# A decoder layer on one core: rotation tables moved from GpSimd to VectorE, operand splits made on 128 partitions, and the lower-part products put last in each step

## The chip, the core and the metric

The kernel runs on one core of one Trainium2 chip. The core has TensorE (matrix products into PSUM, "PE" in the profile, with its weight loads as "PEld"), VectorE ("DVE"), ScalarE ("ACT"), GpSimd ("POOL") and a queue of SyncE ("SP") that issues most of the transfers from HBM. Each engine takes its own instructions in order and waits on semaphores for the others. The metric is the device time of one execution in microseconds, the median of three runs.

## The reference

The reference is one layer of a hybrid decoder for 256 positions and 2048 channels, in float32. One projection `x @ w_in` feeds three token mixers, whose results are gated, merged and projected; two layer norms and a squared-ReLU MLP with 8192 hidden channels follow.

```python
h = jnp.einsum('bsd,dn->bsn', x, w_in)          # 2048 -> 14352 columns
y_a = s5_branch(...)                            # 64 groups of 16 channels, 64 complex states each
y_b = gla_branch(...)                           # 4 heads, chunked gated linear attention
y_c = hgrn2_branch(...)                         # 8 heads, the same with another gate
merged = sum_b sigmoid(gate_b) * (y_b @ w_up_b);  mix = merged @ w_out
x = layer_norm(ALPHA * x + mix);  x = layer_norm(ALPHA * x + square(relu(x @ w1)) @ w2)
```

The part that the change touches most is the S5 branch. Each state p of a group follows s_t = a s_(t-1) + (Bbar u)_t with a complex a = mag * exp(i * theta), and y = Re(C s) + D u. With the state written as a rotation times a slowly varying z, the recurrence becomes a real one: z_t = mag * z_(t-1) + exp(-i theta t) (Bbar u)_t, and s_t = exp(i theta t) z_t. That needs tables of cos(theta t) and sin(theta t) for every state and all 256 positions.

## The kernel before, in words

**Products.** Every large product is made of float32 operands split in two: an upper part rounded to the type `float32r`, and a lower part, the rest. A product is then upper x upper + upper x lower + lower x upper. ScalarE makes the upper part of the weights (`emit_split`, an ACTIVATE at line 129 on a page of 128 x 1024), VectorE the lower (`emit_lower`, a TENSOR_TENSOR at line 107, the raw page less the upper one). The weights come in units of 512 KB, one page each, up to 8 units ahead (`AHEAD`), and each unit is used in two consecutive steps. The split of a unit is placed `LA` = 6 steps ahead of its use.

**Steps.** The program is one list of 1140 steps. A step of kind "rows" has the activations as stationary operand and two 128-deep slices of the unit as moving operand (128 x 512): six matmuls, lines 1341 (upper x upper), 1342 (upper x lower part of the weights) and 1343 (lower x upper). A step of kind "cols" has the weights as stationary operand: per 128-deep slice one matmul of the weights' upper part with both parts of the activations side by side (line 1346, 512 columns) and one of the weights' lower part with the activations' upper part (line 1347, 256 columns), four slices to a step; a kind "low" has the same pairs. There are 752 "rows" steps, 384 "cols" and 4 "low".

**What is woven in.** Everything else (S5, the two attentions, the norms) is written as tasks that are stepped between the steps. `run_tasks(1240, 1240)` lets a task emit instructions only while the estimated VectorE and ScalarE time already emitted (`used`) is under a budget that grows by 1240 ns each step. So the order of the instructions on every engine is fixed by these estimates when the program is built; work on GpSimd is not counted in them. The order on an engine is the order of emission.

**S5.** The 32 pairs of groups are handled in 16 half-blocks `hb` of two. `s5_prepare` scales B and C, transposes them on PE, and copies the result from PSUM into `W` (ScalarE). For each half-block it gathers the inputs `u` and the B rows into stacks of 96 partitions (`RU`, `RB`: three copies of 32 rows each, 12 transfers on SP, lines 463 and 464). ScalarE rounds the stacks (`SU`, `SB`), and VectorE replaces the second third of `SU` and the last third of `SB` by the lower parts (two operations on 32 partitions x 512). One matmul over the 96 rows then is the three-part product (`pb`, line 519: four matmuls of 256 columns).

`s5_tables(hb)` makes cos and sin of all 256 positions from 16 fine and 16 coarse angles by the addition theorems: six operations of 128 x 512 on GpSimd (lines 493 to 498: two products and a difference for the cosine, two products and a sum for the sine). `s5_main` calls it for the next half-block when the matmuls of this one have been issued. Then VectorE rotates `pb` by the tables (eight operations of 128 x 256 at line 107 and two of 128 x 512), scans four rows of 256 (line 543), rotates back, and PE multiplies by C (line 563).

## Time and profile before

| | |
|---|---|
| median of three runs | 1694.33 us (1694.15 to 1695.88) |
| the profiled execution: device time | 1696.22 us |
| the profiled execution: span from first to last instruction | 1694.4 us |
| PE busy | 1671.3 us, 99% of the span, 9396 matmuls |
| VectorE busy | 1190.8 us, 70% |
| ScalarE busy | 825.5 us, 49% |
| GpSimd busy | 161.3 us, 10%, in the first 800 us |
| from HBM | 308.7 MB, 183 GB/s over the span |

An engine's busy share is an average over stages. The matmuls are pipelined: the profile gives each a duration of about 0.39 us, but the next one starts about 0.23 us after it, so what one matmul costs is read from the starts of two neighbours and not from the duration. A wait is put down to the engine and line that ended it. "Granted clock" is the share of TensorE's full clock in a stretch of time.

### The profile page before, as it was taken

To read this page: it belongs to the slowest core of one execution; us is meant where nothing else is said; L and a number is where in the kernel's file an instruction comes from. 1 tells how busy PE (TensorE), PEld (TensorE's weight loads), DVE (VectorE), ACT (ScalarE), POOL (GpSimd) and SP (SyncE) were. 2 spreads that over 40 slices of the span, in tenths; PEclk is the share of its full clock that TensorE was granted. 3 is DMA by queue.
4 is the path that set the end of the run, shared out by engine and by line. 5 is a ranking of instruction groups with operands and counts; after the bars stand their busy time and mean duration, and the time that the engine had idled before them with its cause. 6 is when DMAs were issued, how large, how long until landed. Compare 5 with 4: busy or idle time off the path is not lost.

```text
span 1694.4 us, 24226 instructions
## 1 busy us (share of the span) xinstructions
PE 1671.3 (99%) x9396; PEld 1386.1 (82%) x9396; DVE 1190.8 (70%) x1587; ACT 825.5 (49%) x1166; POOL 161.3 (10%) x121
## 2 busy tenths in 40 slices
PE   9999999999999999999999999999999999999997
PEld 7887788887877877788888888888888888888886
DVE  6968778797998999985575667545555545555556
ACT  5553554564644434435554466454454545464550
POOL 3222022012332332200000000000000000000000
PEclk9999999999999999999999999999999999999999
DMA  9945655564555665676676545655656565656561
GB/s 287 275 145 157 178 177 168 153 194 139 173 180 169 194 196 172 207 221 186 200 263 220 187 150 150 197 188 187 211 179 206 163 213 171 218 163 208 197 233 50
DMA packets 222900, 318.70 MB, mean 188 GB/s; under 512 B 13205, under 2 KB 122129, under 8 KB 222785
## 3 DMA queue, kind: packets, MB, share of 16 engines
q1 hardware_dynamic: 217488, 308.59, 58.3%
q10 hardware_dynamic: 4528, 7.31, 1.3%
q0 software_dynamic: 768, 1.25, 0.5%
q8 instruction: 74, 1.21, 0.3%
q14 instruction: 42, 0.34, 0.1%
HBM read 308.71 MB, written 2.10 MB: 183 GB/s over the span
## 4 chain that ended last, share of the span: by engine, by line
PE 66%; DVE 4%; issue 1%; ACT 0%; DVEq 0%
PE acc L1341 15%; PE acc L1342 15%; PE acc L1343 15%; PE acc L1346 14%; PE acc L1347 7%; DVE pg L107 2%; DVE hf L107 1%; PE m L134 1%; DVE hf L543 1%; PE m L563 1%; DVE pg L118 0%; PE pb L519 0%; ACT pg L129 0%; DVE st L941 0%; DVEq L1403 0%
## 5 line engine op out<-in xcount | busy, mean ns | idle before, releaser
L129 ACT ACTIVATE pg<-pg 128x1024 fp32r<-128x1024 f32 (+2 forms) x604 | 603.1, 1028 | 413.7 <-PE acc L1342 147.0
L107 DVE TENSOR_TENSOR pg<-pg,pg 128x1024 fp32r<-128x1024 f32 (+3 forms) x646 | 749.9, 1188 | 58.9 <-ACT pg L129 32.7
L1341 PE MATMUL acc<-pg,pg 128*128 128x512 f32 x1504 | 595.5, 396 | 2.7 <-DVE pg L107 1.8
L1342 PE MATMUL acc<-pg,pg 128*128 128x512 f32 x1504 | 587.3, 390 | 2.7 <-DVE pg L107 2.7
L1343 PE MATMUL acc<-pg,pg 128*128 128x512 f32 x1504 | 587.0, 390 | 0.2
L1346 PE MATMUL acc<-pg,pg 128*128 128x512 f32 x1552 | 551.9, 400 | 0.0
L1347 PE MATMUL acc<-pg,pg 128*128 128x256 f32 x1552 | 436.6, 281 | 1.9 <-DVE pg L107 1.9
L1346 PEld LDWEIGHTS acc<-pg,pg 128*128 128x128 f32 x1552 | 292.4, 188 | 72.9 <-issue 0.7
L1341 PEld LDWEIGHTS acc<-pg,pg 128*128 128x128 f32 x1504 | 282.8, 188 | 68.4 <-issue 5.8
L1343 PEld LDWEIGHTS acc<-pg,pg 128*128 128x128 f32 x1504 | 282.6, 188 | 61.5 <-DVE pg L107 1.4
L1342 PEld LDWEIGHTS acc<-pg,pg 128*128 128x128 f32 x1504 | 282.9, 188 | 60.6 <-DVE pg L107 5.1
L1347 PEld LDWEIGHTS acc<-pg,pg 128*128 128x128 f32 x1552 | 293.9, 189 | 2.8 <-DVE pg L107 2.3
L129 ACT ACTIVATE hf<-acc 128x256 f32<-128x256 f32 (+2 forms) x103 | 40.0, 388 | 184.5 <-PE acc L1347 179.6
L107 DVE TENSOR_TENSOR pg<-pg,acc 128x512 f32<-128x512 f32 x56 | 38.3, 685 | 121.3 <-PE acc L1343 121.3
L107 DVE TENSOR_TENSOR hf<-acc,hf 128x256 f32<-128x256 f32 (+1 forms) x69 | 29.1, 421 | 131.9 <-ACT hf L129 131.9
L107 DVE TENSOR_TENSOR hf<-hf,hf 128x512 f32<-128x512 f32 (+1 forms) x144 | 106.6, 758 | 4.7 <-ACT hf L129 2.8
L129 ACT ACTIVATE hf<-hf 128x256 f32<-128x256 f32 (+1 forms) x152 | 67.7, 456 | 2.3 <-DMA hf<-pg 0.5
L129 ACT ACTIVATE pg<-acc 128x512 f32<-128x512 f32 x40 | 23.8, 595 | 83.7 <-PE acc L1343 74.5
L107 DVE TENSOR_TENSOR hf<-pb,hf 128x256 f32<-128x256 f32 x128 | 46.5, 414 | 22.8 <-PE pb L519 16.8
L107 DVE TENSOR_TENSOR pg<-hf,pg 128x256 fp32r<-128x256 f32 x84 | 34.7, 421 | 27.7 <-ACT pg L129 27.6
L129 ACT ACTIVATE pg<-m 128x512 fp32r<-128x512 f32 (+2 forms) x35 | 19.6, 559 | 68.0 <-PE m L134 51.8
L543 DVE TENSOR_TENSOR_SCAN hf<-p,hf 128x256 f32<-128x256 f32 x64 | 47.7, 792 | 0.0
(128 smaller groups left out, 641.1 us busy)
## 6 DMA issues: line engine op xcount, KB each, us to landing
pg<-in_w_in_dram SPq DMA_DIRECT2D x224, 512.0 KB, 4.2
pg<-in_w_mlp_in_dram SPq DMA_DIRECT2D x128, 512.0 KB, 4.6
pg<-in_w_mlp_out_dram SPq DMA_DIRECT2D x128, 512.0 KB, 4.0
pg<-in_w_up_dram SPq DMA_DIRECT2D x48, 512.0 KB, 4.7
pg<-in_w_out_dram SPq DMA_DIRECT2D x32, 512.0 KB, 5.5
pg<-in_s_w_glu_dram SPq DMA_DIRECT2D x8, 512.0 KB, 4.7
hf<-pg SPq DMA_DIRECT2D x96, 32.0 KB, 1.9
hf<-hf SPq DMA_DIRECT2D x96, 32.0 KB, 1.9
```

Of the source, the lines that this page charges most:

```text
L107: V.tensor_tensor(o, a, b, op=op)
L129: S.activation(o, a, f, **kw)
L134: T.transpose(ps[:, i * 128:(i + 1) * 128], s, ident)
L543: V.tensor_tensor_scan(z[:, i, :], S5["mag"][:, j:j + 1].to_broadcast([128, 256]), z[:, i, :], 0.0, ALU.mult, ALU.add)
L563: T.matmul(yps[r, 0:256], lhsT=W[:, 2 + ri, r], rhs=m[:, i, :], start=ri == 0, stop=ri == 1)
L1341: T.matmul(ps, lhsT=a[0][:, sl], rhs=wh[:, i, :], start=f, stop=False)
L1342: T.matmul(ps, lhsT=a[0][:, sl], rhs=wl[:, i, :], start=False, stop=False)
L1343: T.matmul(ps, lhsT=a[1][:, sl], rhs=wh[:, i, :], start=False, stop=l)
L1346: T.matmul(ps, lhsT=wh[:, i, n], rhs=a[2], start=f, stop=False)
L1347: T.matmul(ps[:, 0:256], lhsT=wl[:, i, n], rhs=a[0], start=False, stop=l)
```

## The change

Four things are changed.

1. **Products.** In each step the products with the lower part of the weights come last. In a "rows" step the order of the six matmuls was uu, ul, lu, uu, ul, lu (u upper, l lower; activations first) and is uu, lu, uu, lu, ul, ul. In a "cols" step the eight matmuls were 512, 256, 512, 256 ... columns and are four of 512 and then four of 256.
2. **Tables.** `s5_tables` is on VectorE and nothing of it on GpSimd. The fine angles go from 0.5 to 7.5 in place of 0 to 15 (`tvec` has 0.5 added; 8 of its 16 entries are used), the coarse ones are the same 16. One product pair gives the sum and the difference of two angles, so that a table of 16 x 16 is made of products of 16 x 8: per half-block eight operations of 128 x 256, four products and four sums, half of the sums written in reversed order. Places where other tasks may step in (`yield 0`) stand between them.
3. **Rotations.** `pb` holds the real parts of both groups in one buffer and the imaginary parts in the other, so the eight rotations of 128 x 256 become four of 128 x 512.
4. **Parts on 128 partitions.** `s5_prepare` splits `u` and B into upper and lower parts before the gather, on all 128 partitions, once per pair of half-blocks: two ACTIVATEs (`UP`, `BP`) and two subtractions of 128 x 256 on VectorE. The transfers fetch upper or lower rows as each third needs them. The two subtractions of 32 x 512 per half-block are gone.

The step's budget goes from 1240 to 1290 ns.

```diff
+        ts(tvec[:, 0, :], tvec[:, 0, :], 0.5, None, ALU.add)
...
+            UP = half((128, 2, 256), F32R)
+            act(UP[:, 0, :], u, AF.Copy)
...
-            W = half((128, 4, 128))
-            act(W, ps.rearrange("p (b s) -> p b s", b=4), AF.Copy)
+            W, BP = half((128, 2, 128)), half((128, 2, 256), F32R)
+            act(BP[:, 0, :], ps[:, 0:256], AF.Copy)
+            act(W, ps[:, 256:512].rearrange("p (b s) -> p b s", b=2), AF.Copy)
             S5["W", b] = W
+            yield 0.5
+            tt(UP[:, 1, :], u, UP[:, 0, :].bitcast(F32), ALU.subtract)
+            tt(BP[:, 1, :], ps[:, 0:256], BP[:, 0, :].bitcast(F32), ALU.subtract)
...
-                        nc.sync.dma_start(RU[32 * k:32 * k + 32, i, :], u[r])
-                        nc.sync.dma_start(RB[32 * k:32 * k + 32, i, :], W[r, 0:2, :].rearrange("p a b -> p (a b)"))
+                        nc.sync.dma_start(RU[32 * k:32 * k + 32, i, :], UP[r, int(k == 1), :].bitcast(F32))
+                        nc.sync.dma_start(RB[32 * k:32 * k + 32, i, :], BP[r, int(k == 2), :].bitcast(F32))
...
-                tt(SU[32:64], RU[32:64], SU[32:64].bitcast(F32), ALU.subtract)
-                tt(SB[64:96], RB[64:96], SB[64:96].bitcast(F32), ALU.subtract)
...
-        so, co, w = (half((128, 2, 16, 16)) for _ in range(3))
-        G.tensor_tensor(co, coarse(cs), fine(cs), op=ALU.mult)
-        G.tensor_tensor(w, coarse(sn), fine(sn), op=ALU.mult)
-        G.tensor_tensor(co, co, w, op=ALU.subtract)
-        G.tensor_tensor(so, coarse(sn), fine(cs), op=ALU.mult)
-        G.tensor_tensor(w, coarse(cs), fine(sn), op=ALU.mult)
-        G.tensor_tensor(so, so, w, op=ALU.add)
-        free(w)
+        so, co = half((128, 2, 16, 16)), half((128, 2, 16, 16))
+        for o, x1, y1, x2, y2, op1, op2 in ((co, cs, cs, sn, sn, ALU.subtract, ALU.add),
+                                            (so, sn, cs, cs, sn, ALU.add, ALU.subtract)):
+            w = half((128, 2, 2, 16, 8))
+            tt(w[:, 0], coarse(x1), fine(y1), ALU.mult)
+            tt(w[:, 1], coarse(x2), fine(y2), ALU.mult)
+            yield 0
+            tt(o[:, :, :, 8:16], w[:, 0], w[:, 1], op1)
+            tt(o[:, :, :, 7::-1], w[:, 0], w[:, 1], op2)
+            free(w)
+            yield 0
...
-                    T.matmul(pb[i][:, ri, :], lhsT=SB[:, i, ri * 128:(ri + 1) * 128], rhs=SU[:, i, :],
+                    T.matmul(pb[ri][:, i, :], lhsT=SB[:, i, ri * 128:(ri + 1) * 128], rhs=SU[:, i, :],
...
-            for i in range(2):
-                tt(zr[:, i, :], pb[i][:, 0, :], cs[:, i, :], ALU.mult)
-                tt(w1[:, i, :], pb[i][:, 1, :], sn[:, i, :], ALU.mult)
+            tt(zr, pb[0], cs, ALU.mult)
+            tt(w1, pb[1], sn, ALU.mult)
...
-        run_tasks(1240, 1240)
+        run_tasks(1290, 1290)
...
-                T.matmul(ps, lhsT=a[0][:, sl], rhs=wh[:, i, :], start=f, stop=False)
-                T.matmul(ps, lhsT=a[0][:, sl], rhs=wl[:, i, :], start=False, stop=False)
-                T.matmul(ps, lhsT=a[1][:, sl], rhs=wh[:, i, :], start=False, stop=l)
-            elif c.kind == "cols" or i // (nj // 2) == t:
-                T.matmul(ps, lhsT=wh[:, i, n], rhs=a[2], start=f, stop=False)
-                T.matmul(ps[:, 0:256], lhsT=wl[:, i, n], rhs=a[0], start=False, stop=l)
+            for i, kt in kts:
+                a = c.act(kt)
+                T.matmul(ps, lhsT=a[0][:, sl], rhs=wh[:, i, :], start=kt == 0, stop=False)
+                T.matmul(ps, lhsT=a[1][:, sl], rhs=wh[:, i, :], start=False, stop=False)
+            for i, kt in kts:
+                T.matmul(ps, lhsT=c.act(kt)[0][:, sl], rhs=wl[:, i, :], start=False, stop=kt == nk - 1)
+        else:
...
+            for i, kt in kts:
+                T.matmul(ps, lhsT=wh[:, i, n], rhs=c.act(kt)[2], start=kt == 0, stop=False)
+            for i, kt in kts:
+                T.matmul(ps[:, 0:256], lhsT=wl[:, i, n], rhs=c.act(kt)[0], start=False, stop=kt == nk - 1)
```

How the program's order moves is shown at two places. The first is the first "cols" step on PE. `acc` is the accumulator, the second name (`pg_112`, `pg_144`) the activations with both parts, `pg_368` the upper and `pg_369` the lower part of the weights. Before:

```order
L1346 MATMUL acc_406<-pg_112,pg_368 128x512
L1347 MATMUL acc_406<-pg_112,pg_369 128x256
L1346 MATMUL acc_406<-pg_112,pg_368 128x512
L1347 MATMUL acc_406<-pg_112,pg_369 128x256
L1346 MATMUL acc_406<-pg_144,pg_368 128x512
L1347 MATMUL acc_406<-pg_144,pg_369 128x256
L1346 MATMUL acc_406<-pg_144,pg_368 128x512
L1347 MATMUL acc_406<-pg_144,pg_369 128x256
```

And with the change, the same step and the one after it:

```order
L1355 MATMUL acc_414<-pg_112,pg_368 128x512 x2
L1355 MATMUL acc_414<-pg_144,pg_368 128x512 x2
L1357 MATMUL acc_414<-pg_112,pg_369 128x256 x2
L1357 MATMUL acc_414<-pg_144,pg_369 128x256 x2
L1355 MATMUL acc_424<-pg_112,pg_368 128x512 x2
L1355 MATMUL acc_424<-pg_144,pg_368 128x512 x2
L1357 MATMUL acc_424<-pg_112,pg_369 128x256 x2
L1357 MATMUL acc_424<-pg_144,pg_369 128x256 x2
```

The first use of the lower part moves from the second to the fifth place of a step, and short matmuls follow short ones.

The second place is VectorE in the middle of S5, in the stage where the attentions are over: one half-block's rotations, scans and the lower parts of the weights between them (`pg_...<-pg_...,pg_...` of 128 x 1024; the scans are written SCALAR_TENSOR_TENSOR with `p`, and `pg_4852`, `pg_5159` belong to the merge). Before:

```order
L107 TENSOR_TENSOR hf_6127<-pb_0_6110,hf_5779 128x256
L107 TENSOR_TENSOR hf_6127<-pb_1_6111,hf_5779 128x256
L107 TENSOR_TENSOR hf_6126<-hf_6126,hf_6127 128x512
L107 TENSOR_TENSOR pg_6167<-pg_5995,pg_6166 128x1024
L543 SCALAR_TENSOR_TENSOR hf_6125<-p_602,hf_6125 128x256 x2
L107 TENSOR_TENSOR pg_6188<-pg_6038,pg_6187 128x1024
L107 TENSOR_TENSOR hf_6198<-hf_6096,hf_6198 32x512
L107 TENSOR_TENSOR hf_6199<-hf_6097,hf_6199 32x512
L107 TENSOR_TENSOR pg_6212<-pg_6056,pg_6211 128x1024
L543 SCALAR_TENSOR_TENSOR hf_6126<-p_602,hf_6126 128x256 x2
```

With the change, the tables of the next half-block (`hf_6439`, `hf_6438`) stand ahead of the rotations of this one:

```order
L107 TENSOR_TENSOR hf_6440<-pg_578 128x256
L107 TENSOR_TENSOR hf_6440<-pg_577 128x256
L107 TENSOR_TENSOR hf_6439<-hf_6440 128x32x8 x2
L107 TENSOR_TENSOR pg_6403<-pg_6276,pg_6402 128x1024
L107 TENSOR_TENSOR hf_6458<-pg_577,pg_578 128x256
L107 TENSOR_TENSOR hf_6458<-pg_578,pg_577 128x256
L107 TENSOR_TENSOR hf_6438<-hf_6458 128x32x8 x2
L107 TENSOR_TENSOR hf_6469<-pb_0_6432,hf_6188 128x512
L107 TENSOR_TENSOR hf_6471<-pb_1_6433,hf_6187 128x512
L107 TENSOR_TENSOR pg_6454<-pg_6298,pg_6453 128x1024
L107 TENSOR_TENSOR hf_6469<-hf_6469,hf_6471 128x512
L107 TENSOR_TENSOR hf_6470<-pb_1_6433,hf_6188 128x512
```

Eight table operations of 128 x 256 come in, the rotations are half as many and twice as wide, and the two subtractions on 32 partitions are no longer among them.

More of the change, by code (lines that the diff above doesn't have):

```diff
@@ L447, in s5_prepare @@
             yield from wait_for(("u", b // 4))
-            yield from room("hf", 1, 4)
+            yield from room("hf", 3, 4)
+            u = uT[b // 4][:, b % 4, :]
+            UP = half((128, 2, 256), F32R)
+            act(UP[:, 0, :], u, AF.Copy)
             ps = psm()
@@ L468, in s5_prepare @@
                 act(SB, RB, AF.Copy)
-                yield 0.5
-                tt(SU[32:64], RU[32:64], SU[32:64].bitcast(F32), ALU.subtract)
-                tt(SB[64:96], RB[64:96], SB[64:96].bitcast(F32), ALU.subtract)
                 free(RU, RB)
-                yield 1.5
+                yield 1
                 S5["stack", hb] = SU, SB
+            free(UP, BP)
     SIN2 = 6.2831845
@@ L486, in fine @@
         def fine(x):
[L487 removed]
+            return x[:, 0, 2 * hb:2 * hb + 2, 0:8].unsqueeze(2).to_broadcast([128, 2, 16, 8])
         def coarse(x):
[L490 removed]
+            return x[:, 1, 2 * hb:2 * hb + 2, :].unsqueeze(3).to_broadcast([128, 2, 16, 8])
         sn, cs = S5["sn"], S5["cs"]
[L492 to L499 removed]
+        so, co = half((128, 2, 16, 16)), half((128, 2, 16, 16))
[9 more added lines that the diff above has]
+            yield 0
         S5["tab", hb] = tuple(x.rearrange("p i a b -> p i (a b)") for x in (so, co)), (so, co)
@@ L505, in s5_main @@
         yield from room("hf", 4)
-        s5_tables(0)
+        yield from s5_tables(0)
         for hb in range(16):
@@ L523, in s5_main @@
                 yield from room("hf", 3, 4)
-                s5_tables(hb + 1)
+                yield from s5_tables(hb + 1)
             yield from room("hf", 3, 3)
             zr, zi, w1 = half(), half(), half()
-            for i in range(2):
-                tt(zr[:, i, :], pb[i][:, 0, :], cs[:, i, :], ALU.mult)
-                tt(w1[:, i, :], pb[i][:, 1, :], sn[:, i, :], ALU.mult)
+            tt(zr, pb[0], cs, ALU.mult)
+            tt(w1, pb[1], sn, ALU.mult)
             yield 0
             tt(zr, zr, w1, ALU.add)
-            for i in range(2):
-                tt(zi[:, i, :], pb[i][:, 1, :], cs[:, i, :], ALU.mult)
+            tt(zi, pb[1], cs, ALU.mult)
             yield 0
-            for i in range(2):
-                tt(w1[:, i, :], pb[i][:, 0, :], sn[:, i, :], ALU.mult)
+            tt(w1, pb[0], sn, ALU.mult)
             tt(zi, zi, w1, ALU.subtract)
@@ L562, in s5_main @@
                 for ri, m in ((0, sre), (1, cs)):
-                    T.matmul(yps[r, 0:256], lhsT=W[:, 2 + ri, r], rhs=m[:, i, :],
+                    T.matmul(yps[r, 0:256], lhsT=W[:, ri, r], rhs=m[:, i, :],
                              start=ri == 0, stop=ri == 1)
@@ L1334, in trunk_kernel @@
         wh, wl = (a.rearrange("p a b -> p (a b)").rearrange("p (k n) -> p k n", n=wn) for a in (hi, lo))
-        for i in range(nj):
-            kt = ku * kpu + j * nj + i
-            f, l = kt == 0, kt == nk - 1
-            a = c.act(kt)
-            if c.kind == "rows":
-                sl = slice(t * 128, (t + 1) * 128)
-                T.matmul(ps, lhsT=a[0][:, sl], rhs=wh[:, i, :], start=f, stop=False)
-                T.matmul(ps, lhsT=a[0][:, sl], rhs=wl[:, i, :], start=False, stop=False)
-                T.matmul(ps, lhsT=a[1][:, sl], rhs=wh[:, i, :], start=False, stop=l)
-            elif c.kind == "cols" or i // (nj // 2) == t:
-                n = slice(t * 128, (t + 1) * 128) if c.kind == "cols" else slice(0, 128)
-                T.matmul(ps, lhsT=wh[:, i, n], rhs=a[2], start=f, stop=False)
-                T.matmul(ps[:, 0:256], lhsT=wl[:, i, n], rhs=a[0], start=False, stop=l)
+        kts = [(i, ku * kpu + j * nj + i) for i in range(nj)]
+        if c.kind == "rows":
+            sl = slice(t * 128, (t + 1) * 128)
+            for i, kt in kts:
[5 more added lines that the diff above has]
+        else:
+            if c.kind == "low":
+                kts = [(i, kt) for i, kt in kts if i // (nj // 2) == t]
+            n = slice(t * 128, (t + 1) * 128) if c.kind == "cols" else slice(0, 128)
+            for i, kt in kts:
+                T.matmul(ps, lhsT=wh[:, i, n], rhs=c.act(kt)[2], start=kt == 0, stop=False)
+            for i, kt in kts:
+                T.matmul(ps[:, 0:256], lhsT=wl[:, i, n], rhs=c.act(kt)[0], start=False, stop=kt == nk - 1)
         uses_left[k] -= 1
```

3 lines of the change are left out of this document (removed).

## The prediction

> **What bounds the kernel now.** I read the page first, then the starts of neighbouring matmuls in the timeline, then the waits that end PE's idle time, and last VectorE's groups by stage.
>
> ```profile
> span 1694.4 us, 24226 instructions
> PE 1671.3 (99%) x9396; PEld 1386.1 (82%) x9396; DVE 1190.8 (70%) x1587; ACT 825.5 (49%) x1166; POOL 161.3 (10%) x121
> L1347 PE MATMUL acc<-pg,pg 128*128 128x256 f32 x1552 | 436.6, 281 | 1.9 <-DVE pg L107 1.9
> ```
>
> PE is the bound nearly everywhere: 23 us of the span are without a matmul. So the change can gain in two ways only: the matmuls themselves come closer together, or PE's waits go. The last row counts the short matmuls: 1552, four to a step, so 388 groups of four pairs.
>
> What a matmul costs is the distance of starts. A "cols" stretch, eleven pairs of one long and one short matmul:
>
> ```profile
> 1039.80 0.40 PE L1346 MATMUL acc<-pg,pg 128*128 128x512 f32 x1
> ...
> 1043.69 0.40 PE L1346 MATMUL acc<-pg,pg 128*128 128x512 f32 x1
> ```
>
> 3.89 us for 11 pairs, 0.3536 us a pair. A "rows" stretch of long matmuls alone, 53 distances:
>
> ```profile
> 899.82 0.39 PE L1341 MATMUL acc<-pg,pg 128*128 128x512 f32 x1
> ...
> 911.83 0.39 PE L1343 MATMUL acc<-pg,pg 128*128 128x512 f32 x1
> ```
>
> 12.01 us for 53, 0.2266 us each. And four short ones in a row, S5's products, with what follows them:
>
> ```profile
> 120.95 0.64 PE L519 MATMUL pb<-hf,hf 96*128 96x256 f32 x4
> 121.43 0.40 PE L1346 MATMUL acc<-pg,pg 128*128 128x512 f32 x1
> ```
>
> 0.48 us for four, 0.12 us each. Long and short taken apart are 0.2266 + 0.12 = 0.3466 us, 7 ns less than the mixed pair.
>
> PE's waits are few. In the S5 stage the idle time is 1.6 and 1.9 us in these two stretches, at VectorE 90% busy:
>
> ```profile
> 500.00:550.00 50.00, 48.39 (x221) 38.04 (x220) 45.32 (x60) 21.82 (x23) 14.20 (x9) 1.00 0.58 173
> 600.00:650.00 50.00, 48.13 (x223) 38.39 (x222) 45.46 (x63) 21.11 (x24) 12.63 (x9) 1.00 0.51 155
> ```
>
> Two earlier waits are longer, and the first is followed by slow matmuls:
>
> ```profile
> 90.36 0.40 PE L1346 MATMUL acc<-pg,pg 128*128 128x512 f32 x1
> 92.69 0.39 PE L1347 MATMUL acc<-pg,pg 128*128 128x256 f32 x1 [1.93 <-DVE pg L107]
> ...
> 93.33 0.63 PE L1346 MATMUL acc<-pg,pg 128*128 128x512 f32 x1
> ...
> 96.53 0.42 PE L1346 MATMUL acc<-pg,pg 128*128 128x512 f32 x1
> ```
>
> ```profile
> 147.65 0.39 PE L1343 MATMUL acc<-pg,pg 128*128 128x512 f32 x1
> 151.01 0.98 PE L634 MATMUL m<-pg,pg 128*32 128x16 f32 x64 [2.98 <-DVE pg L107]
> ```
>
> ```profile
> 93.20:96.50 3.30, 3.30 (x12) 2.82 (x11) 3.30 (x5) 0.00 (x0) 2.33 (x1) 0.50 0.48 129
> ```
>
> The first costs 2.33 us in place of some 0.24, 2.1 us. Behind it five pairs take 3.20 us, 0.64 each and not 0.354: the granted clock is 0.50 there (the last row's third number from the end), another 1.4 us. The second waits about 3.0 us, and I price its aftermath as at the first, 4.4 us together. By the Trainium skill ("TensorE: Matmul & The Clock Gate", the HAM clock gate) the clock falls to half after an idle window of about 3.4 us; here a wait of 2.3 us was enough, so the trace differs. By the page's rule the waits would cost 2.1 and 3.0 us alone, and the gain below would be some 2 us smaller.
>
> **The change part by part.** *Order in "cols" steps.* Three of four distances become long after long (0.2266), three short after short (0.12), and one of each transition remains, together the mixed pair of 0.3536: 0.680 + 0.360 + 0.354 = 1.394 us a step, for 4 x 0.3536 = 1.414. 0.0206 x 388 = **8.0 us** gained. Bounds: nothing, if a short matmul behind a short one takes 0.127; 4 x 0.007 x 388 = 10.9 us, if the transitions too fall to the unmixed distances. "Rows" steps have only long matmuls in either order and gain nothing in distance.
>
> *Order as slack.* The lower part is first used at the fifth place of a step and not at the second, 3 x 0.2266 = 0.68 us later; each wait for a lower part of the weights may shrink by that much. The other lower part, of the activations, is used earlier, but it was made long before, outside the first 14 steps; there the two cancel and I take nothing.
>
> *GpSimd's tables gone.* GpSimd's operations stretch VectorE's. One pair of scans beside them, and one without:
>
> ```profile
> 629.99 2.04 POOL L497 TENSOR_TENSOR hf<-pg,pg 128x512 f32<-128x512 f32 x1
> ```
>
> ```profile
> 497.33 1.27 DVE L543 TENSOR_TENSOR_SCAN hf<-p,hf 128x256 f32<-128x256 f32 x2
> ...
> 631.03 3.18 DVE L543 TENSOR_TENSOR_SCAN hf<-p,hf 128x256 f32<-128x256 f32 x2
> ```
>
> VectorE's groups from 480 to 650 us, five half-blocks (20 scans):
>
> ```profile
> L107 DVE TENSOR_TENSOR pg<-pg,pg 128x1024 fp32r<-128x1024 f32 x56 | 74.5, 1342 | 0.2
> L107 DVE TENSOR_TENSOR hf<-hf,hf 128x512 f32<-128x512 f32 x39 | 30.7, 810 | 0.4
> L107 DVE TENSOR_TENSOR hf<-pb,hf 128x256 f32<-128x256 f32 x46 | 16.7, 413 | 7.5 <-issue 5.0 <-PE pb L519 2.5
> L543 DVE TENSOR_TENSOR_SCAN hf<-p,hf 128x256 f32<-128x256 f32 x20 | 16.4, 862 | 0.0
> L107 DVE TENSOR_TENSOR hf<-hf,hf 32x512 fp32r<-32x512 f32 x10 | 8.3, 833 | 0.3
> ```
>
> And the same kinds from 800 us on, with GpSimd idle:
>
> ```profile
> L107 DVE TENSOR_TENSOR pg<-pg,pg 128x1024 fp32r<-128x1024 f32 x311 | 369.1, 1220 | 20.3 <-ACT pg L129 18.5 <-issue 0.9 <-PE acc L1343 0.7
> L107 DVE TENSOR_TENSOR pg<-pg,acc 128x512 f32<-128x512 f32 x56 | 38.3, 685 | 121.3 <-PE acc L1343 121.3
> L107 DVE TENSOR_TENSOR pg<-hf,pg 128x256 fp32r<-128x256 f32 x84 | 34.7, 421 | 27.7 <-ACT pg L129 27.6
> ```
>
> The stretch per half-block: (1342 - 1220) x 56 = 6.8 us, (810 - 685) x 39 = 4.9, (862 - 635) x 20 = 4.5; 16.2 us over five, 3.2 us each. It goes.
>
> *What VectorE gets and loses per half-block.* Eight table operations at 0.421: +3.4 us. Their operands repeat elements and half the sums are written backwards, which no row shows; I take the plain row, with twice that (+6.7) as the other end. Rotations: 8 x 0.413 becomes 4 x 0.685, -0.6. Splits: 2 x 0.833 becomes half of 2 x 0.421, -1.2. Net +1.6 of work and -3.2 of stretch: **VectorE is relieved by some 1.6 us per half-block**. The stage's idle time on PE, 3.5 us in the two rows above, goes with it and with the 0.68 us of slack: **3.5 us**, bounds 0 and 3.8.
>
> *The two early waits.* Ahead of the one at 90 us VectorE did S5's scaling beside GpSimd's first tables:
>
> ```profile
> 87.83 0.28 DVE L444 COPY s5eb<-pg 64x64 f32<-64x64 f32 x2
> 88.03 1.10 DVE L112 TENSOR_SCALAR s5ec<-pg,gmask 128x128 f32<-128x128 f32 x1
> 89.14 1.08 DVE L444 COPY s5eb<-pg 64x64 f32<-64x64 f32 x2
> ```
>
> The same copies take 0.28 and 1.08 us. With the scaling stretched alike, some 2 us are lost in these and the next, as much as the wait; the new tables stand behind them in the order. The wait and its half clock go: **3.6 us**. At 147 us the wait is for an attention product that stands behind a backlog of VectorE work, only part of it stretched; the S5 work remains ahead of it. I take half of 4.4: **2.3 us**, bounds 0 and 4.4.
>
> *What hides the rest.* ScalarE gets two instructions more per pair of half-blocks and is 49% busy. The gathers on SP, twelve per half-block as before, now also wait for VectorE's subtractions, and weight transfers are queued behind them:
>
> ```profile
> pg<-in_w_in_dram SPq DMA_DIRECT2D x224, 512.0 KB, 4.2
> ```
>
> A transfer lands in 4.2 us and up to eight units, 16 steps of about 1.4 us, are fetched ahead; a wait of a few us for VectorE is covered, and without that cover it would cost what VectorE is behind, some 5 us at most per gather. The budget of 1290 ns lets tasks emit 4% more per step, which is about what the tables take; by the order S5 keeps its pace.
>
> **Sum.** 8.0 + 3.5 + 3.6 + 2.3 = 17.4 us. The profiled execution of 1696.2 us (span 1694.4 and 1.8 around it) becomes 1678.8. It lies 1.9 us above the median of the runs, so the median is **1677 us**. The ends: all terms at their best, 10.9 + 3.8 + 3.6 + 4.4 = 22.7, give 1672; the product order alone 1686.
>
> **The rivals.** *Weight loads bound the short matmuls* (the other side). Behind a short matmul the next weight load has little time:
>
> ```profile
> L519 PEld LDWEIGHTS pb<-hf,hf x64: 187/190/193, 120.8 to 744.1; 96*128 96x128 f32 x64
> ```
>
> If a load held the path for its 0.19 us, each of the 3 x 388 = 1164 short-after-short distances would be 0.19, +81 us: 1677 + 81 = 1758. It decides from 0.135 us on, where 1164 x 15 ns eat the 17.4. Against it: these very loads, of 190 ns, stand in front of matmuls 0.12 apart. By the Trainium skill (the same page, LDWEIGHTS) a load of 128 columns takes 107 ns, which would leave the 0.12 standing; the trace's 190 is then latency.
>
> *VectorE becomes the bound in S5.* With table operations at 0.84, +3.4 per half-block turns the relief into +1.8; from about 0.62 on it is a loss. In 450 to 650 us VectorE has little left (45 of 50), six half-blocks give +11 us, against 8.0 from the products: 1697. For it: no row shows such operands. Against: all forms of one size cost alike in the rows above.
>
> *No gain in distance.* Short after short at 0.127: 1685. S5's four had 96 rows and different accumulators; here all four add to the same one.
>
> *The waits stay*, since other work is late in their place, or new ones come with the new order: 1686.
>
> **How the numbers follow.** Forecast 0.66; no gain in distance 0.13; waits stay 0.13; VectorE bound 0.05; weight loads 0.03. The range holds the forecast and the two middle rivals: 1670 to 1688. A measurement of this kernel tells 0.2%, 3.4 us, from no change. Faster: 0.66 + 0.13 + 0.13 = 0.92, less 0.03 for both middle cases at once with a new wait, which lands within 0.2%: 0.89. VectorE's 1697 is within it too at its value, but with its spread more often slower: 0.02 and 0.03. So within 0.2%: 0.05; slower: 0.06.
>
> **What would show it.** In the changed kernel's timeline, short matmuls start 0.12 us apart and a "cols" step takes 1.39 us; lower parts on VectorE are at 1.22 us in the S5 stage too, and the scans near 0.63; table operations are at 0.42; PE is busy 49.5 or more of 50 us from 450 to 650; no half clock after 90 us. Short matmuls at 0.127 or more, table operations above 0.6, or a PE idle time of over 3 us in the S5 stage would make the prediction wrong.

## The result, and the profile after

The changed kernel takes 1679.34 us (median of four runs, 1679.19 to 1679.82), beside 1695.11 us (1694.15 to 1697.32) for the kernel before in the same comparison. The ratio is 0.9904, with a 95% interval from 0.9891 to 0.9918: faster by about 1%. The forecast was 1677. The profiled execution took 1679.49 us. The head of its page:

```profile
span 1677.4 us, 24130 instructions
PE 1661.9 (99%) x9396; PEld 1384.6 (83%) x9396; DVE 1159.5 (69%) x1636; ACT 828.5 (49%) x1183; POOL 15.6 (1%) x25
```

GpSimd has lost its 146 us, and VectorE, which took the tables over, is busy for 31 us less than before, not more.

Where the time went is read from the starts of the steps. The 1140 steps have the same kinds in both kernels, so the start of a step's first matmul can be set beside its counterpart (a gain is how much shorter a stage has become, counted from step 0, which starts 0.08 us later here):

| start of step | before, us | after, us | gained in the stage | what is in the stage |
|---|---|---|---|---|
| 0 | 7.40 | 7.48 | | |
| 60 | 105.10 | 101.33 | 3.85 | the wait at 90 us |
| 120 | 204.37 | 196.93 | 3.68 | the wait at 147 us |
| 280 | 463.93 | 456.15 | 0.34 | "cols" and "rows" steps |
| 480 | 762.01 | 747.82 | 6.41 | S5, "rows" steps only |
| 1139 | 1681.93 | 1664.88 | 2.85 | S5 is all but done: product order alone |

**"Cols" steps.** The timeline of PE, two steps and the next one's start, the first behind a stretch of "rows" steps:

```profile
1092.05 1.07 PE L1355 MATMUL acc<-pg,pg 128*128 128x512 f32 x4
1092.95 0.64 PE L1357 MATMUL acc<-pg,pg 128*128 128x256 f32 x4
1093.42 1.09 PE L1355 MATMUL acc<-pg,pg 128*128 128x512 f32 x4
1094.35 0.63 PE L1357 MATMUL acc<-pg,pg 128*128 128x256 f32 x4
1094.83 1.09 PE L1355 MATMUL acc<-pg,pg 128*128 128x512 f32 x4
```

The first step takes 1.37 us: four long matmuls in 0.90, four short ones in 0.47. The second takes 1.41: its short ones need 0.48, as forecast, but its four long ones 0.93, so 0.233 us each and not 0.227. Later steps are all like the second. Over the 343 "cols" steps that neither kernel disturbs, the mean is 1.4124 us before and 1.4019 after: 0.0105 gained and not 0.0206. The slowness lasts into the "rows" matmuls behind the last "cols" step:

```profile
1136.92 0.40 PE L1346 MATMUL acc<-pg,pg 128*128 128x512 f32 x1
...
1139.01 0.39 PE L1347 MATMUL acc<-pg,pg 128*128 128x512 f32 x1
```

Nine distances from 1136.92 to 1139.01 are 0.232 us each.

**The S5 stage.** PE, PEld, VectorE, ScalarE, GpSimd by stretch, then the granted clock:

```profile
500.00:550.00 50.00, 50.00 (x233) 40.09 (x232) 46.35 (x73) 23.64 (x28) 0.00 (x0) 1.00 0.58 169
600.00:650.00 50.00, 50.00 (x230) 40.09 (x229) 43.86 (x66) 21.64 (x25) 0.00 (x0) 1.00 0.65 203
```

The 1.6 and 1.9 us of idle time on PE are gone. VectorE's groups from 480 to 650 us:

```profile
L107 DVE TENSOR_TENSOR pg<-pg,pg 128x1024 fp32r<-128x1024 f32 x56 | 67.9, 1217 | 1.5 <-ACT pg L129 1.4
L107 DVE TENSOR_TENSOR hf<-hf,hf 128x512 f32<-128x512 f32 x37 | 24.4, 685 | 0.2
L107 DVE TENSOR_TENSOR hf<-pb,hf 128x512 f32<-128x512 f32 x24 | 15.9, 682 | 3.1 <-PE pb L528 3.1
L549 DVE TENSOR_TENSOR_SCAN hf<-p,hf 128x256 f32<-128x256 f32 x20 | 12.4, 672 | 0.0
L107 DVE TENSOR_TENSOR hf<-hf 128x256 f32<-128x256 f32 x23 | 8.8, 420 | 0.2
...
L107 DVE TENSOR_TENSOR hf<-pg,pg 128x256 f32<-128x256 f32 x12 | 4.5, 418 | 0.0
```

Lower parts went from 1342 to 1217 ns, the operations of 512 from 810 to 685, a scan from 862 to 672. The last two rows are table operations: sums, half of them written backwards, and products of repeated elements, all at the price of a plain operation.

**The first 160 us.** The timeline of PE at the places of the two old waits, and at a new one:

```profile
90.37 1.09 PE L1355 MATMUL acc<-pg,pg 128*128 128x512 f32 x4
91.30 0.64 PE L1357 MATMUL acc<-pg,pg 128*128 128x256 f32 x4
...
112.78 0.74 PE L528 MATMUL pb<-hf,hf 96*128 96x256 f32 x4 [1.50 <-ACT hf L129]
113.36 1.09 PE L1355 MATMUL acc<-pg,pg 128*128 128x512 f32 x4
...
144.98 0.61 PE L1349 MATMUL acc<-pg,pg 128*128 128x512 f32 x2
145.52 0.74 PE L640 MATMUL m<-pg,pg 128*32 128x16 f32 x64
```

At 90 us and at 145 us nothing waits now (L640 at 145.52 is the attention product that waited 2.98 us, the first of its kind, in step 88 of both kernels). At 112.78 S5's products wait 1.50 us for ScalarE's rounding of a stack; the four long matmuls behind it run at full speed.

### The profile page after: what moved, and what is told of

Read it like the earlier page. It is cut to its first block, busy times and chain, and to the rows that moved or that the text cites. A ratio compares the mean times of both kernels' runs of the same rounds, so it can differ in the third digit from the quotient of the medians.

```text
span 1677.4 us, 24130 instructions
## 1 busy us (share of the span) xinstructions
PE 1661.9 (99%) x9396; PEld 1384.6 (83%) x9396; DVE 1159.5 (69%) x1636; ACT 828.5 (49%) x1183; POOL 15.6 (1%) x25
## 4 chain that ended last, share of the span: by engine, by line
PE 97%; DVE 2%; DMA 1%; ACT 0%; SPq 0%; issue 0%; DVEq 0%; ACTq 0%
PE acc L1346 21%; PE acc L1355 21%; PE acc L1347 20%; PE acc L1349 20%; PE acc L1357 11%; DVE pg L107 1%; PE m L134 1%; PE m L569 1%; PE m L640 1%; PE pb L528 0%; DMA pg<-in_w_in_dram 0%; DVE pg L118 0%; PE m L696 0%; PE m L697 0%; PE m L694 0%; PE m L651 0%
## 5 line engine op out<-in xcount | busy, mean ns | idle before, releaser
L107 DVE TENSOR_TENSOR pg<-pg,pg 128x1024 fp32r<-128x1024 f32 (+2 forms) x646 | 729.6, 1155 | 60.7 <-ACT pg L129 32.9
L1346 PE MATMUL acc<-pg,pg 128*128 128x512 f32 x1504 | 594.5, 395 | 0.3 <-ACT pg L129 0.3
L1347 PE MATMUL acc<-pg,pg 128*128 128x512 f32 x1504 | 587.1, 390 | 0.4 <-DVE pg L107 0.3
L1349 PE MATMUL acc<-pg,pg 128*128 128x512 f32 x1504 | 464.1, 390 | 0.0
L1355 PE MATMUL acc<-pg,pg 128*128 128x512 f32 x1552 | 424.5, 395 | 0.1
L1346 PEld LDWEIGHTS acc<-pg,pg 128*128 128x128 f32 x1504 | 282.4, 188 | 62.9 <-issue 6.2
L1349 PEld LDWEIGHTS acc<-pg,pg 128*128 128x128 f32 x1504 | 282.3, 188 | 60.6 <-DVE pg L107 0.4
L1347 PEld LDWEIGHTS acc<-pg,pg 128*128 128x128 f32 x1504 | 282.6, 188 | 58.0 <-DVE pg L107 2.7
L1355 PEld LDWEIGHTS acc<-pg,pg 128*128 128x128 f32 x1552 | 266.2, 189 | 37.0 <-issue 0.7
L1357 PEld LDWEIGHTS acc<-pg,pg 128*128 128x128 f32 x1552 | 237.9, 189 | 33.4 <-DVE pg L107 0.3
L1357 PE MATMUL acc<-pg,pg 128*128 128x256 f32 x1552 | 247.0, 281 | 0.0
L107 DVE TENSOR_TENSOR hf<-hf,hf 128x512 f32<-128x512 f32 x112 | 74.0, 685 | 0.8
L107 DVE TENSOR_TENSOR pg<-m,pg 128x512 fp32r<-128x512 f32 (+1 forms) x34 | 23.4, 689 | 37.5 <-ACT pg L129 20.2
L107 DVE TENSOR_TENSOR hf<-pb,hf 128x512 f32<-128x512 f32 x64 | 42.4, 682 | 7.8 <-PE pb L528 7.8
```

Source lines behind the costliest of these rows:

```text
L107: V.tensor_tensor(o, a, b, op=op)
L1346: T.matmul(ps, lhsT=a[0][:, sl], rhs=wh[:, i, :], start=kt == 0, stop=False)
L1347: T.matmul(ps, lhsT=a[1][:, sl], rhs=wh[:, i, :], start=False, stop=False)
L1349: T.matmul(ps, lhsT=c.act(kt)[0][:, sl], rhs=wl[:, i, :], start=False, stop=kt == nk - 1)
L1355: T.matmul(ps, lhsT=wh[:, i, n], rhs=c.act(kt)[2], start=kt == 0, stop=False)
L1357: T.matmul(ps[:, 0:256], lhsT=wl[:, i, n], rhs=c.act(kt)[0], start=False, stop=kt == nk - 1)
```

## The experiments

Each run was compared with runs of the kernel before on the same chip; ratios are to that kernel. Its median was 1694.9 to 1695.8 us in these comparisons, so the times of two different runs can be set side by side to about 1 us.

**1. The product order alone.** The kernel before, with the changed order of products and nothing else:

```diff
-            for i in range(nj): ...   # upper, lower, upper, lower
+            for i, kt in kts: ...     # upper parts of the weights
+            for i, kt in kts: ...     # then lower parts
```

> The kernel before, with the order of the products of the change and nothing else (tables on GpSimd, old rotations and splits, budget 1240). Theory 1 (the waits come from GpSimd stretching VectorE, the order gives only the distance of the matmuls and 0.68 us of slack per wait): a cols step 1.402 us as after the change, 4.1 us in all; of the waits at 90, 147 and 450 to 650 us perhaps 2 to 3 us; 1688 us, PE idle 500 to 650 us still above 2 us, half clock after 90 us stays. Rival (the order's slack is what takes the waits away): 1681 to 1683 us, no idle time of PE from 450 to 650 us.

Measured: 1689.69 us, ratio 0.9965 (0.9954 to 0.9977). The waits stay; the timeline of PE:

```profile
93.38 0.74 PE L1351 MATMUL acc<-pg,pg 128*128 128x256 f32 x4 [1.40 <-DVE pg L107]
...
149.27 0.74 PE L634 MATMUL m<-pg,pg 128*32 128x16 f32 x64 [2.97 <-DVE pg L107]
```

The first is 0.53 us shorter than before (1.93), because the lower part is now needed later in its step, and no half clock follows it. The second is unchanged. From 450 to 650 us PE's waits still sum to 3.0 us (3.9 before), and they are of two kinds. The longest in the kernel before, 1.87 us at 636.59, is for a lower part of the weights; it is 1.20 here, 0.67 less, as the slack should have it. The next one is not for a lower part. VectorE and PE in the kernel before:

```profile
506.56 0.68 DVE L107 TENSOR_TENSOR pg<-acc,pg 128x512 f32<-128x512 f32 x1
```

```profile
507.29 0.50 PE L1341 MATMUL acc<-pg,pg 128*128 128x512 f32 x1 [1.01 <-DVE pg L107]
```

It ends 0.05 us after VectorE has read out an accumulator (`acc`), and it is 1.02 us long here. So the order gives 5 us: the distances and some slack. It shortens the waits and takes none of the two long ones away.

**2. Everything but the order.** The changed kernel with the old order of products (the diff above, reversed).

> The changed kernel with the old order of the products. Theory 1: the waits stay away without the slack, only the 4.1 us of distances come back: 1683 to 1684 us, PE busy 49.5 of 50 us from 450 to 650 us. Rival (slack): waits of lower parts come back, 1688 us or more.

Measured: 1683.63 us, ratio 0.9929 (0.9914 to 0.9944). PE is busy 50.00 of 50 us in all four windows from 450 to 650, and no wait is left at 90 or 147 us. The order is worth 1683.63 - 1679.34 = 4.3 us in the changed kernel, and 0.0105 x 388 = 4.1 us are distances. The two parts alone give 5.4 and 11.5 us, both at once 15.8: they add up but for about 1 us.

**3. Half as many changes between long and short.** In the second step of a unit the short matmuls come first, so that runs of eight alternate:

```diff
+            shorts_first = c.kind == "cols" and t == 1 and kts[0][1] > 0
...
+            if shorts_first:
+                shorts()
+                longs()
```

> The changed kernel; in the second step of each unit of kind cols the four short matmuls come first and the four long ones last, so that shorts of two steps stand together and longs of two steps too: half as many changes between long and short. Theory A (each run of shorts leaves the next ten or so long matmuls at 234 ns in place of 227, however it is cut): 1679 us, same within 1 us, longs still 230 ns or more in the mean. Theory B (a fixed price for each change of kind): half of the excess goes, 0.024 us per pair of steps, 4.7 us: 1674.5 us, cols step 1.389 us.

Measured: 1677.24 us, ratio 0.9892 (0.9876 to 0.9909), 2.1 us below the changed kernel: between the two theories. So small a difference of times could be no change; the distances show what moved. The timeline of PE:

```profile
1100.54 1.12 PE L1362 MATMUL acc<-pg,pg 128*128 128x256 f32 x8
1101.49 2.00 PE L1357 MATMUL acc<-pg,pg 128*128 128x512 f32 x8
1103.33 0.64 PE L1362 MATMUL acc<-pg,pg 128*128 128x256 f32 x4
```

Eight short ones take 0.95 us, 0.119 each; eight long ones 1.84, 0.230 each. Inside the run of eight only the first five are slow (means after 1000 us: 233, 236, 228, 233 and 231 ns, then 227). So the loss is neither in the change itself (which would cost one distance) nor in every long matmul: four long ones behind four short ones lose some 22 ns together (means of 233.5, 233.8, 232.8 and 228.4 in the changed kernel are 21.7 over four times 226.7), and eight behind eight lose 27, all in the first five. The loss grows far less than the run.

**4. No short matmuls.** In the changed kernel, the products with the weights' lower parts in "cols" steps are left out:

```diff
-            for i, kt in kts:
-                T.matmul(ps[:, 0:256], lhsT=wl[:, i, n], ...)
```

> The changed kernel without the short products (weights' lower part by activations' upper part) in the cols steps; that part of the result is left out. Theories A and B (short matmuls slow the long ones behind them): longs 227 ns apart, a cols step 0.907 us, 388 x (1.402 - 0.907) = 192 us less, 1487 us. Theory C (the cols operands themselves make longs 234 ns): 0.936 us a step, 1498 us.

Measured: 1533.94 us, a single execution. A stretch of "cols" steps in the timeline of PE:

```profile
1049.73 4.47 PE L1355 MATMUL acc<-pg,pg 128*128 128x512 f32 x19
```

Less one modelled duration of 0.39 these are 18 distances in 4.08 us: 0.2267. The same operands, without short neighbours, are as fast as in "rows" steps, so standing behind short ones makes the long ones slow. The time is 47 us above the expected 1487, and that is a finding of its own. PE now waits, mostly in the first 450 us; its largest wait, in total, times and longest:

```profile
PE acc L1355 <- DVE pg L107: 18.0, 8, 3.8
```

These eight waits are not for lower parts: each ends 0.05 us after VectorE has read out an accumulator, as the one of 2.63 us at 228.56, behind this operation:

```profile
228.09 0.42 DVE L107 TENSOR_TENSOR pg<-acc,hf 128x256 f32<-128x256 f32 x1
```

With a tenth of PE's work gone, VectorE comes to the accumulators late behind its other work. All waits of PE sum to 36 us (4 in the changed kernel), and the granted clock is 0.50 in six stretches, 27 us together, in which PE is busy for 23; by an estimate from these numbers half clock costs some 12 us, so waits and clock together are most of the 47.

**5. The tables back on GpSimd.** The changed kernel with the old `s5_tables`; the budget of 1290 ns stays:

```diff
-            tt(w[:, 0], coarse(x1), fine(y1), ALU.mult)   # and seven more on VectorE
+        G.tensor_tensor(co, coarse(cs), fine(cs), op=ALU.mult)   # and five more on GpSimd
```

> The changed kernel with the tables back on GpSimd as before (six operations of 128 x 512 per half-block), everything else of the change kept. Theory 1 (GpSimd's operations stretch VectorE's, and that makes PE wait): lower parts at 1.3 us and scans at 0.8 us in the mean from 480 to 650 us, waits of PE at 90, 147 and 450 to 650 us return in part (new order's slack and cheaper rotations keep some away): 1685 to 1690 us. Rival (VectorE's own work decides, and the tables add to it): faster than the change, under 1679 us.

Measured: 1705.36 us, ratio 1.0054 (1.0036 to 1.0073): slower than the kernel before, and worse than was expected. VectorE's groups from 480 to 650 us:

```profile
L107 DVE TENSOR_TENSOR pg<-pg,pg 128x1024 fp32r<-128x1024 f32 x52 | 74.2, 1446 | 2.1 <-issue 1.6 <-ACT pg L129 0.5
...
L544 DVE TENSOR_TENSOR_SCAN hf<-p,hf 128x256 f32<-128x256 f32 x20 | 22.1, 1167 | 0.0
```

Scans take 1167 ns (672 in the changed kernel), lower parts 1446 (1217), and one wait of PE reaches 4.18 us at 516 us. The run mixes two things, GpSimd's work and a budget in which that work isn't counted; run 9 parts them.

**6. Useless work on GpSimd.** The changed kernel, with 24 products of 128 x 128 per half-block added on GpSimd, whose results nobody reads:

```diff
+        for k in range(4):
+            for x, y in ((cs, cs), (sn, sn), (cs, sn), (sn, cs), (cs, cs), (sn, sn)):
+                G.tensor_tensor(scr, c(x), f(y, k), op=ALU.mult)
```

> The changed kernel, and beside the tables on VectorE GpSimd computes products of the same inputs into a buffer that nobody reads (24 operations of 128 x 128 per half-block); no engine waits for them. Theory 1 (stretch by sharing): VectorE's operations on two SBUF inputs get longer by some 3 us per half-block, PE waits from 450 to 650 us for several us: 1686 us or more. Rival (the tables from GpSimd came late, and VectorE waited for them): nobody waits for these, so 1679 us.

Measured: 1687.96 us, ratio 0.9955 (0.9940 to 0.9970), 8.6 us above the changed kernel. GpSimd is busy 280 us with these products, almost twice as long as it was with the tables. Two waits of ScalarE are put down to them (4.1 us at 301 and 4.0 at 404), in a stage in which PE is busy throughout, and none in the S5 stage; so there their place beside VectorE is the cost. By stretch:

```profile
450.00:500.00 50.00, 48.72 (x221) 39.31 (x220) 49.77 (x66) 22.84 (x29) 45.18 (x62) 1.00 0.55 166
500.00:550.00 50.00, 46.14 (x203) 36.18 (x203) 49.83 (x64) 23.96 (x28) 45.53 (x58) 0.97 0.56 166
...
600.00:650.00 50.00, 50.00 (x232) 40.10 (x231) 43.88 (x65) 21.31 (x26) 0.00 (x0) 1.00 0.63 193
```

Where GpSimd is busy 45 of 50 us VectorE is full and PE idles; where it is idle, all is as in the changed kernel. VectorE's groups from 450 to 550 us:

```profile
L107 DVE TENSOR_TENSOR pg<-pg,pg 128x1024 fp32r<-128x1024 f32 x34 | 45.8, 1356 | 0.0
L107 DVE TENSOR_TENSOR hf<-hf,hf 128x512 f32<-128x512 f32 x21 | 17.0, 836 | 0.1
...
L107 DVE TENSOR_TENSOR hf<-pb,hf 128x512 f32<-128x512 f32 x12 | 7.9, 677 | 0.0
...
L107 DVE TENSOR_TENSOR hf<-pg,pg 128x256 f32<-128x256 f32 x6 | 3.5, 619 | 0.0
```

Operations with both inputs in SBUF are stretched by 11 to 48% (1217, 685 and 418 ns without GpSimd); those with one input in PSUM (`pb`) not at all (682). By the Trainium skill ("GPSIMD Engine Reference", 1. Specifications) GpSimd contends with VectorE instructions that have two SBUF inputs, or run in a 2-port mode; for two inputs the trace agrees, and puts a price to it. Copies with a single input are stretched too (`s5eb`, from 185 to 296 ns in the mean), and no run here shows in which mode they ran.

**7. The budget at 1250 ns** in place of 1290.

```diff
-        run_tasks(1290, 1290)
+        run_tasks(1250, 1250)
```

> The changed kernel with a budget of 1250 ns per step in place of 1290, so S5 goes on more slowly. VectorE has room in both (under 47 of 50 us), so 1679 us within 2 us; if the budget itself brought part of the gain, 1683 us or more.

Measured: 1678.16 us, ratio 0.9897 (0.9882 to 0.9912): 1.2 us less, within what can't be told from no change. PE is busy 50.00 of 50 us from 100 to 150, so the new wait at 112 us is not there. The wider budget is no source of the gain.

**8. The old rotations and splits.** The changed kernel with eight rotations of 128 x 256 and with the stacks' lower parts made on 32 partitions after the gather; tables on VectorE and product order stay:

```diff
-            tt(zr, pb[0], cs, ALU.mult)
+            for i in range(2):
+                tt(zr[:, i, :], pb[i][:, 0, :], cs[:, i, :], ALU.mult)
...
+                tt(SU[32:64], RU[32:64], SU[32:64].bitcast(F32), ALU.subtract)
```

> The changed kernel with the old rotations (eight of 128 x 256) and the old splits (two of 32 x 512 per half-block); tables on VectorE and the new order kept. VectorE gets 1.6 us more per half-block, some 26 us in all, 46 of 50 us busy from 450 to 650 us. If that still fits beside PE: 1679 to 1681 us; if VectorE is at its limit, as the rival of the prediction has it: 1685 us or more.

Measured: 1678.81 us, ratio 0.9900 (0.9885 to 0.9915). No difference. VectorE is at 39.7 to 46.7 of 50 us from 450 to 650 and PE at 50.00 throughout: what the two parts save, VectorE no longer needs. VectorE is busy 1179.7 us in this run and 1190.8 in the kernel before: with the same rotations and splits, it is busy for 11 us less when it makes the tables itself than when GpSimd makes them beside it.

**9. Run 5 with the old budget** of 1240 ns (the diff of run 5, and the one line of run 7 with 1240).

> The tables go back to GpSimd as in the run before that came to 1705 us, and the budget goes back from 1290 to 1240 ns; the product order, the wider rotations and the splits on 128 partitions stay. Theory A: the 16 us by which that run was slower than the run with the order alone (1689.7) came from the budget, which let the tasks emit more per step than VectorE, stretched by GpSimd, could do; then this kernel comes to 1687 to 1691, PE idles about 1.5 us in three of the windows from 450 to 650 us, and lower parts there still take 1.34 us or more. Theory B: GpSimd's tables beside the new rotations and splits are the cause, whatever the budget; then it stays at 1700 or more, with waits of 3 to 4.6 us on PE.

Measured: 1692.45 us, ratio 0.9981 (0.9972 to 0.9990). The budget accounts for 12.9 of the 15.7 us between run 5 and run 1. That fits tasks let in that VectorE, stretched by GpSimd, could not do in time: with the tables on VectorE, budgets of 1290 and 1250 differ by 1.2 us (run 7). Some of the 12.9 is half clock: it lasts 13.7 us in the trace of run 5 before the last 10 us and 3.4 in that of run 9. The other 2.8 us, a little more than theory A allowed, were not traced to a part; PE's waits from 450 to 650 us sum to 6.5 us here and to 3.0 in run 1. Two waits of this run, in the timeline of PE:

```profile
541.91 0.63 PE L1341 MATMUL acc<-pg,pg 128*128 128x512 f32 x1 [3.31 <-DVE pg L107]
542.34 0.63 PE L1342 MATMUL acc<-pg,pg 128*128 128x512 f32 x1
...
573.98 0.74 PE L1344 MATMUL acc<-pg,pg 128*128 128x512 f32 x2 [1.68 <-DVE pg L107]
574.56 0.40 PE L1341 MATMUL acc<-pg,pg 128*128 128x512 f32 x1
574.79 0.40 PE L1342 MATMUL acc<-pg,pg 128*128 128x512 f32 x1
```

After 3.31 us the matmuls start 0.43 us apart, at half clock; after 1.68 us they are soon 0.23 apart, at full clock.

**10. Runs 3 and 7 together:** long and short in runs of eight, and the budget at 1250.

> The changed kernel with the second step of each cols unit turned round (runs of eight long and eight short matmuls) and the budget at 1250. Theory: the two small gains stand in different places (the distances of the matmuls after 450 us, and the wait near 111 us) and add up: 1679.3 less 2.1 and 1.2, 1676.0. Rival: the wait near 111 us depends on chance in the order of the tasks and another one of its size comes up; then 1677.2, as with the halved changes alone.

Measured: 1676.04 us (1675.69 to 1676.34), ratio 0.9885 (0.9868 to 0.9901). The two add up as forecast. It is the lowest time of a kernel that leaves no work out, 3.3 us below the changed kernel, which is just at the bound of what can be told from no change.

**11 and 12. Shorter weight loads for the short matmuls.** The changed kernel, with 64 and then 32 columns of weights (and rows of output) in the short products of "cols" steps; the rest of these products is left out:

```diff
+                if c.kind == "cols" and kt < nk - 1:
+                    T.matmul(ps[0:64, 0:256], lhsT=wl[:, i, t * 128:t * 128 + 64], ...)   # or 32
```

> The changed kernel, where each short matmul of a cols step (but those of a chunk's last units) loads 64 columns of weights instead of 128 and writes 64 rows: half of the lower products is left out. Theory L: the long matmuls behind a run of short ones are slow (233 in place of 227 ns) because the short ones' weight loads, 190 ns each at 120 ns apart, leave the loads behind; with smaller loads they are not, a cols step falls from 1.402 to 1.38 us, and the time to 1670. Theory M: the short matmuls themselves leave something behind, whatever they load; then the longs stay at 233, a step at 1.40, and the time at 1679.

> As the run with 64 columns of weights in the short products of cols steps, with 32 columns and 32 rows of output: three quarters of those lower products are left out. Loads of 128, 64 and 32 columns take 188, 134 and 109 to 110 ns in the traces, and the short matmuls start 116 to 119 ns apart. Theory L1 (a load that is longer than its matmul leaves a backlog that the long ones pay): 110 is below 116, so no backlog is left: the long matmuls are 227 ns apart from the first one, a step takes 1.37 us, and the time is about 1669. Theory L2 (the cost goes with the number of loaded columns): 15 ns a step were saved by 64 columns, so 32 more save 7.5 ns, a step takes 1.380 us, and the time is about 1672.5. Theory M (what is left is from the matmuls themselves): the step stays at 1.387 us and the time at 1675.

Measured, a single execution each: 1675.41 us with 64 columns, 1678.23 with 32. The loads, by their groups, with 64 and with 32 columns:

```profile
L1358 PEld LDWEIGHTS acc<-pg,pg 128*64 128x64 f32 x1436 | 180.0, 134 | 52.9 <-DVE pg L107 0.2
```

```profile
L1358 PEld LDWEIGHTS acc<-pg,pg 128*32 128x32 f32 x1436 | 154.8, 108 | 69.9 <-DVE pg L107 0.2
```

They last 134 and 108 ns in place of 188: 64 columns fewer take 54 ns off and another 32 take 26, so 0.83 ns a column stand on some 81 ns that do not go with the columns. Two starts of a step each, with 64 and with 32 columns:

```profile
1100.59 1.08 PE L1355 MATMUL acc<-pg,pg 128*128 128x512 f32 x4
...
1101.97 1.08 PE L1355 MATMUL acc<-pg,pg 128*128 128x512 f32 x4
```

```profile
1099.91 1.08 PE L1355 MATMUL acc<-pg,pg 128*128 128x512 f32 x4
...
1101.30 1.09 PE L1355 MATMUL acc<-pg,pg 128*128 128x512 f32 x4
```

Means after 1000 us: with 64 columns four long ones take 923.6 ns and four short ones 463.6, together 1.387 us; with 32 columns 929.6 and 469.6, together 1.399, nearly the 1.402 of full loads. A long load that leaves a backlog would be mended by both, and more by the second. So neither theory of the loads stands: by what short matmuls slow the long ones behind them stays open.

## Why the prediction was right, and where it was not

The time was forecast to 2.3 us (1677 against 1679.34), and the sum of 17.4 us stands against 17.1 between the first and the last step. The terms are less good than the sum; two errors cancel, and that the sum came so close is luck. (By its own rows the prediction's terms are 8.1, 3.5, 3.5 and 2.2 us; the slips of 0.1 us change nothing.)

- **Order in "cols" steps: 8.0 us forecast, 4.1 measured.** The mis-sized term, and the sign that missed: a "cols" step takes 1.40 us and not 1.39. Short behind short is 0.117 to 0.120, as taken from S5's products, so the rival that has them at 0.127 and the one with bound weight loads are both wrong in their mechanism. What failed is the other distance: 0.2266 for long behind long was read in "rows" steps, where no short matmul is near, and behind short ones it is 0.233. The time lost there was inside the forecast's own bounds (0 to 10.9); run 3 shows its length, run 4 its source. The row that gives it stood in the timeline of the kernel before, behind four of S5's short products:

```profile
489.30 0.64 PE L519 MATMUL pb<-hf,hf 96*128 96x256 f32 x4
489.77 0.40 PE L1341 MATMUL acc<-pg,pg 128*128 128x512 f32 x1
...
490.70 0.39 PE L1342 MATMUL acc<-pg,pg 128*128 128x512 f32 x1
```

  Four distances of long matmuls take 0.93 us there too, where four of 0.2266 would take 0.91. The pair of 0.3536 in the old order is, in the mean after 1000 us, a long one of 0.236 and a short one of 0.117: all of its loss was in the long one.
- **The S5 stage: 3.5 us forecast, 6.4 measured**, outside its bounds of 0 and 3.8. The mechanism holds: runs 2 and 8 keep the gain without the order, the rotations or the splits; run 6 takes it back with GpSimd's work alone, though with almost twice as much of it. No wait of VectorE in the kernel before is put down to GpSimd, so late tables were not the cause. PE's waits there are for lower parts (2.1 us in two waits) and for accumulators that VectorE has to read out (1.8 us in three); the new order's slack shortens the first kind alone (run 1), and a relieved VectorE takes both away (run 2). The size was read from PE's idle time, which counts from a matmul's modelled end (0.39 us) and not from the 0.227 at which the next could start. In distances of starts, the five largest waits of "rows" matmuls in this stage cost 4.6 us over the undisturbed pace, where the waits by idle time sum to 3.9, and 37 delays of 0.01 to 0.16 us, hardly seen as idle, cost 3.1; afterwards there are no large ones and 26 small ones, 1.85 us. That is 5.9 of the 6.4.
- **The wait at 90 us: 3.6 us forecast**, 3.8 measured up to step 60, of which 0.3 is distance. Run 1 shows that slack alone would have shortened it to 1.40 us, which is enough to keep the clock.
- **The wait at 147 us: 2.3 us forecast**, as half of 4.4. It went altogether; the "rows" steps of that stage gained 5.3 us. The "cols" steps lost 1.6, most of it in the new wait at 112 us, of which the prediction had no trace: net 3.7. Run 7 has the wait away by another budget, and run 8 by the old parts, so it depends on the order of emission; that it comes from the additional rounding is not shown.
- **The tables' price** of 0.421 us, the step with no row behind it, was 0.418 to 0.420. VectorE's bound in S5 therefore never came near. The relief per half-block came from the end of the stretch, as argued; the scans, at 0.67 and not 0.635, are the one row that it missed a little, since the 1.27 us was that of two scans that overlap.
- **What was costed at nothing** (more rounding on ScalarE, gathers that wait for subtractions) stayed at nothing in the S5 stage; run 8, which undoes both, makes no difference.
- **The step from the profiled execution to the median** was wrong by most of the 2.3 us. For the profiled execution the forecast was 1678.8, and it took 1679.49. Another 1.9 us were taken off, because the profiled execution of the kernel before lay that far above the median; with the change it lies 0.15 us above. The 1.9 us look like half clock behind the waits that went. Of 13 executions of the kernel before, set beside run 9, those with a mean granted clock of 0.997 took 1694.0 to 1694.5 us, those with 0.996 1695.3 to 1696.0, and those with 0.995 1697.2 to 1697.7; the four of the changed kernel all have 0.998. So the kernel before loses more or less to half clock from one execution to the next, and the changed kernel does not.

## What to carry to other kernels

Work on an idle engine is not free: GpSimd's table operations cost VectorE more time than it takes to make the tables itself (run 8), so price such work by the stretch of the operations beside it, and count it in whatever budget sets the order. Read the cost of a matmul, and of a wait, from the starts of neighbours in the very mixture in which it will run, and look whether the trace already has such a place; a distance from a uniform stretch, or an idle time that counts from a modelled end, can each be off by half of the gain. When one part relieves an engine, other parts with the same aim may be worth nothing: test them one by one.

## What the runs showed of the hardware

- About five to nine long matmuls behind a run of short ones start 224 to 237 ns apart instead of 227, in a recurring pattern (233, 236, 228, 233, 231); the cost is 21 to 23 ns for four long ones behind four short and 27 for eight behind eight. It is not in their operands (run 4), and not in the length of the short ones' weight loads alone (runs 11 and 12). Nor does it belong to short matmuls only: in the "rows" steps of the kernel before, the distances behind the wait of 1.01 us that ends at 507.29 are 341, 240, 235, 233, 236, 224, 231, 236, 228, 232 and 231, and then 227; behind S5's products at 489.77 they are 233, 236, 228, 233 and 231, and then 227. It looks like one sequence in which the pace comes back after an interruption, entered at different places. Its mechanism is open.
- A wait of 1.93 us of idle time was followed by half clock (before, at 92.69), as were those of 2.97 and 3.31; waits of 1.40, 1.50 and 1.68 us were not. But the length of a wait does not decide alone: in run 4 a wait of 2.63 us was not followed by half clock. In the clock records of all traces the granted clock changes only at whole multiples of 3.413 us after a run's first record. PE's busy time, then the clock: the window of the kernel before in which the first wait lies (the next one is at 0.50); then the wait of run 4 and its two windows:

```profile
89.73:93.15 3.42, 1.49 (x9) 1.00 0.00 0
```

```profile
228.56 2.83 PE L1355 MATMUL acc<-pg,pg 128*128 128x512 f32 x11 [2.63 <-DVE pg L107]
```

```profile
224.27:227.68 3.41, 1.66 (x8) 1.00 0.83 211
227.68:231.10 3.42, 2.54 (x11) 1.00 0.43 127
```

  The first wait lies in one window, with 1.93 us of idle time; the second straddles two, with 1.75 and 0.88 us of idle time. Over all runs, up to the last 10 us of each, every one of the 14 windows at full clock in which PE was idle for 1.89 us or more was followed by half clock, and none with 1.75 or less. By the Trainium skill ("TensorE: Matmul & The Clock Gate", Part 1: The HAM clock gate) the clock falls after an idle window of about 3.4 us, and the window is free-running; the traces agree with both (the first record stands 4.4 to 7.4 us behind the first instruction, and no wait moves the later ones) and show that little more than half of it idle is enough. So a wait of 1.93 us may cost another 1.4 us or more, as at 92.69, or nothing, depending on where it falls.
- An operation on VectorE whose input repeats elements or whose output runs backwards costs what the plain one does: 418 to 420 ns for 256 elements of float32.
